# A macaron decoder block on one core: the last pair's sums in place, stores ahead of weights, and three smaller moves of order

## The chip, the cores and the metric

The kernel runs on one core of a Trainium2 chip. The metric is the device time of one execution in microseconds (us). Before the change three executions took 1988.55, 1992.07 and 1992.52 us, so the median is 1992.07. Engines are called PE (TensorE, matmuls), PEld (its weight loads), DVE (VectorE), ACT (ScalarE), POOL (GpSimd) and SP (SyncE, which here issues most DMA transfers).

## The reference

One layer over 1024 tokens of width 1024, all in float32:

```
h = x + 0.5 * swiglu(rms(x), w1a, w3a, w2a)          # hidden width 2816
u = rms(h);  q, k, v, p, gates = split(u @ w_in)     # 3*768 + 512 + 2*1024 columns
yA = dilated_attention(rope(q), rope(k), v) @ w_a    # 12 heads of 64, three dilations
yB = pool(p: trailing means of 2, 4, 8, 16 minus p, per-group map, scale) @ w_b
h = h + (sigmoid(gA) * yA + sigmoid(gB) * yB) @ w_o
h = h + 0.5 * swiglu(rms(h), w1b, w3b, w2b)
out = rms(h)
```

with `swiglu(x) = (silu(x @ w1) * (x @ w3)) @ w2`.

## The kernel before

Every float32 operand of a large product is split into a high part (ACT copies it to the narrower matmul type) and a low part (DVE or POOL subtracts the high part from the original), and each product is three matmuls: high by high, high by low, low by high (`three`). Large products are computed as 2 x 2 blocks by a scheme of seven products instead of eight. `Quad` holds one such block of a weight matrix: `operand(m)` forms the weight sums (lines 343 to 354) and splits them (lines 301 on ACT and 304 on DVE or POOL), `run(m)` issues the 12 matmuls of a product, 2.72 us of PE, in the order 1, 6, 2, 7, 5, 4, 3.

Stages, by the span of the profile: an entry up to 72 us; the up products of the first SwiGLU up to 457; its down products up to 684; an entry, then the projection w_in ("mix") from 723 to 1082; attention with the pool branch and the gates; the product with w_o up to about 1310; then the second SwiGLU, up from 1364 to 1756 and down to 1976.

Up products. A `Pair` is two quads, w1 and w3, for two of the 22 tiles of the hidden width. `a_out` and `b_out` take the finished banks and build silu(a) * b in two tiles of 128 x 1024, y_0 and y_1 (tag `tmp`, three buffers). `finish` then makes the left sums for the down products, y_0 + y_1 (`gb`), two differences (`gd`) and the sum of two halves (`e`), and spills seven pieces of 256 KB to DRAM (`gs_...`). `up` runs ten pairs and then an eleventh whose order is written by hand.

Down products. `Down` runs seven products, each in six steps: five steps of 24 matmuls (5.44 us of PE) and one of 12. `load(i)` (line 610) brings the left sum of step i back from DRAM, into a `tmp` buffer or one of tag `row`; `begin(i)` takes the weights of w2, forms their difference or sum on DVE (line 646, `s_f1w...`), and splits both sides (line 625 on ACT, 629 on DVE or POOL; tiles `bhi`, `blo`, `ahi`, `alo`). `multiply` issues the matmuls (line 663). Steps 0 and 1 are begun at the end of the up products, step 2 is loaded at the start of `Down.run`, and from then on step i loads i + 3 and begins i + 2.

Weights come through one `Stream`, `raws`: seven buffers of 512 KB, loaded in a fixed order by SP (lines 67 and 69). `get` takes the next tile, `back(n)` returns n buffers, which at once issues the next loads. SP issues its transfers in program order, and one that has to wait for its buffer holds up those behind it. Blocks of q, k and v are loaded by four transfers of 128 KB each, one for each index of the first dimension (line 67).

Mix. 19 quads, of kinds qk, v, pool and gate. `Mix.out` takes the finished banks, and for a gate applies the sigmoid (line 947) right behind the vector operation. Small generators, one step per product, do the rest beside the products, in the loop over k: `rotate` and `turn` for q, k and v, `window` for the pooled means, `store` for the gates (line 956), and `split_late`, which splits weights needed later (pool_w, w_a and w_b, w_o; lines 1067 to 1073) and stores the parts to DRAM (line 1077).

At the end of mix SP loads what attention and the pool branch need: q, k, v, gates, and four `pool_in` tiles (line 1547) in the order 2, 3, 0, 1. The pool branch's matmuls are line 1561 (`yp`), in the same order.

W_o. 14 steps. Behind the last sums the residual rows h (`h_again`) are stored to DRAM (line 1878), squared on ACT (line 257), and scaled in place by DVE (line 265), after which PE transposes them (line 379). The first four weights of the second SwiGLU are loaded in the loop at step `STEPS - 5`, by `raws.load()`.

Of the kernel before, what the change touches and what calls it, by code (L numbers as in the profile page):

```python
# [13 lines left out]
OP = mybir.AluOpType  # L14
# [32 lines left out]
class Stream:  # L47
# [7 lines left out]
    def load(self):  # L55
        while self.n_loaded < min(self.end, self.n_back + self.depth):
# [70 lines left out]
def tile_block(  # L127
# [189 lines left out]
    class Quad:  # L317
# [39 lines left out]
        def run(self, m):  # L357
# [8 lines left out]
            if m == 3:  # L366
# [86 lines left out]
    class Pair:  # L453
# [72 lines left out]
        def finish(self):  # L526
# [20 lines left out]
            spill(6, d[:, highs])  # L547
            spill(5, d[:, lows])

    def up(sv, sums, between, at_end, begun):  # L550


        for j in range(NPAIR - 1):
# [15 lines left out]
            q.finish()  # L569
        with tc.manual_schedule():  # L570
# [3 lines left out]
            for k, (w, m, out) in enumerate(items):  # L574
                if k + 2 < n:
                    items[k + 2][0].operand(items[k + 2][1])
                res.append(w.run(m))
# [14 lines left out]
    class Down:  # L592
# [3 lines left out]
        def __init__(self, name, sums, dp):  # L596
            self.name, self.sums, self.dp = name, sums, dp
# [3 lines left out]
            self.half_tile = None  # L601
# [5 lines left out]
        def load(self, i, alloc=tmp):  # L607
# [25 lines left out]
        def begin(self, i):  # L633
            m, s = self.steps[i]
            pr = DOWN[m]
            size = self.size(i)
            for kn in pr.loads:
                self.held[kn, s] = raws.get()
            if len(pr.right) == 1:
                srcs = [self.held[pr.right[0], s]]  # L640
            else:
                x, y, op = pr.right
                srcs = []
                for a in range(size):
                    t = self.half_tile("s", f"w{i}_{a}").rearrange("p (a c) -> p a c", a=1)
                    ve.tensor_tensor(t, self.held[x, s][:, a:a + 1], self.held[y, s][:, a:a + 1], op=op)  # L646
                    srcs.append(t)
            w = self.split("b", srcs, i)
            for kn in pr.drops:
# [1427 lines left out]
```

## Time and profile before

| what | value |
|---|---|
| median of three runs | 1992.07 us |
| profiled execution, its own time | 1990.87 us |
| its span, first to last instruction | 1989.1 us |
| mean granted TensorE clock | 0.991 |
| PE / DVE / ACT / POOL busy | 97% / 67% / 38% / 37% |
| DMA moved | 333.57 MB, mean 168 GB/s |

A window's row gives the stretch, then the busy time of PE, PEld, DVE, ACT and POOL with their instruction counts, then the mean granted clock of PE (1.00 is full speed), the share of time in which the core's 16 DMA engines were busy, and the rate in GB/s. A row of waits names the engine, the tile and line that waited, what ended the wait, and then the total in us, how often, and the longest. "SPq" is SP's queue of transfers. A row of transfers gives the count, the size of one and the median time from issue to landing.

### The profile page before, as it was taken

To read this page: it belongs to the slowest core of one execution; us is meant where nothing else is said; L and a number is where in the kernel's file an instruction comes from. 1 tells how busy PE (TensorE), PEld (TensorE's weight loads), DVE (VectorE), ACT (ScalarE), POOL (GpSimd) and SP (SyncE) were. 2 spreads that over 40 slices of the span, in tenths; PEclk is the share of its full clock that TensorE was granted. 3 is DMA by queue.
4 is the path that set the end of the run, shared out by engine and by line. 5 is a ranking of instruction groups with operands and counts; after the bars stand their busy time and mean duration, and the time that the engine had idled before them with its cause. 6 is when DMAs were issued, how large, how long until landed. Compare 5 with 4: busy or idle time off the path is not lost. (4 is left out here: it accounts for less than half of the span.)

```text
span 1989.1 us, 25124 instructions
## 1 busy us (share of the span) xinstructions
PE 1927.1 (97%) x8966; PEld 1585.2 (80%) x8966; DVE 1334.4 (67%) x2014; ACT 764.0 (38%) x1361; POOL 726.8 (37%) x555
## 2 busy tenths in 40 slices
PE   8999999998999999999998999999999999989997
PEld 7788888886888877788877888877888888868885
DVE  7766556656776775657784786768666556567776
ACT  5333333333344442334445663253323333333343
POOL 4333333331222344444544365534333333322221
PEclk9999999999999999999999999999999999999998
DMA  5323322335466527665668897653333223354664
GB/s 209 126 97 117 117 85 101 133 104 203 140 223 216 196 87 232 219 225 180 230 218 288 229 260 261 260 188 113 120 106 133 80 90 123 126 182 136 205 204 147
DMA packets 147581, 333.57 MB, mean 168 GB/s; under 512 B 20736, under 2 KB 41472, under 8 KB 145920
## 3 DMA queue, kind: packets, MB, share of 16 engines
q1 hardware_dynamic: 139104, 309.12, 46.0%
q10 hardware_dynamic: 8352, 22.85, 3.4%
q8 instruction: 71, 1.16, 0.3%
q14 instruction: 54, 0.44, 0.1%
HBM read 229.61 MB, written 102.30 MB: 167 GB/s over the span
## 5 line engine op out<-in xcount | busy, mean ns | idle before, releaser
L663 PE MATMUL d_f<-bhi_f,ahi_f 128*128 128x512 f32 x616 | 242.4, 393 | 10.4 <-ACT ahi_f L625 8.7
L663 PE MATMUL d_f<-bhi_f,alo_f 128*128 128x512 f32 x616 | 242.3, 393 | 3.0 <-POOL alo_f L629 1.9
L663 PE MATMUL d_f<-blo_f,ahi_f 128*128 128x512 f32 x616 | 241.0, 391 | 0.0
L629 POOL TENSOR_TENSOR alo_f<-g_f,ahi_f 128x512 fp32r<-128x512 f32 x70 | 97.4, 1408 | 317.1 <-ACT ahi_f L625 317.1
L312 PE MATMUL u_mixm<-xhi_t_mix,wc_mixm 128*128 128x512 f32 x608 | 195.4, 392 | 1.4 <-POOL wc_mixm L304 1.3
L312 PE MATMUL u_mixm<-xhi_b_mix,wc_mixm 128*128 128x512 f32 x456 | 150.8, 396 | 6.5 <-DVE y_m L939 5.0
L663 PEld LDWEIGHTS d_f<-bhi_f,ahi_f 128*128 128x128 f32 x616 | 116.6, 189 | 36.5 <-ACT ahi_f L625 10.4
L663 PEld LDWEIGHTS d_f<-bhi_f,alo_f 128*128 128x128 f32 x616 | 116.3, 189 | 31.4 <-POOL alo_f L629 5.4
L663 PEld LDWEIGHTS d_f<-blo_f,ahi_f 128*128 128x128 f32 x616 | 116.4, 189 | 24.0
L312 PEld LDWEIGHTS u_mixm<-xhi_t_mix,wc_mixm 128*128 128x128 f32 x608 | 113.8, 188 | 26.8 <-POOL wc_mixm L304 2.9
L312 PE MATMUL u_mixm<-xlo_t_mix,wc_mixm 128*128 128x512 f32 x304 | 118.4, 389 | 0.0
L304 POOL TENSOR_TENSOR wc_mixm<-s_mixm,wc_mixm 128x512 fp32r<-128x512 f32 x52 | 73.4, 1414 | 102.6 <-ACT wc_mixm L301 90.2
L312 PEld LDWEIGHTS u_mixm<-xhi_b_mix,wc_mixm 128*128 128x128 f32 x456 | 86.3, 189 | 26.9 <-issue 6.8
L312 PE MATMUL u_mixm<-xlo_b_mix,wc_mixm 128*128 128x512 f32 x228 | 89.4, 392 | 0.0
L625 ACT ACTIVATE ahi_f<-g_f 128x1024 fp32r<-128x1024 f32 x84 | 81.8, 974 | 4.9 <-DMA g_f<-gs_f 4.9
L301 ACT ACTIVATE wc_mixm<-s_mixm 128x512 fp32r<-128x512 f32 x76 | 47.0, 629 | 94.5 <-DVE s_mixm L345 45.9
L625 ACT ACTIVATE bhi_f<-s_f2w 128x512 fp32r<-128x512 f32 x55 | 32.9, 628 | 104.3 <-DVE s_f2w L646 96.6
L304 POOL TENSOR_TENSOR wc_mixm<-raw,wc_mixm 128x512 fp32r<-128x512 f32 x40 | 58.8, 1475 | 31.4 <-ACT wc_mixm L301 31.4
L1799 PE MATMUL wo<-w_o,o_hi 128*128 128x512 f32 x224 | 70.2, 395 | 0.0
L625 ACT ACTIVATE bhi_f<-s_f1w 128x512 fp32r<-128x512 f32 x55 | 32.9, 629 | 96.9 <-DVE s_f1w L646 92.2
L312 PEld LDWEIGHTS u_mixm<-xlo_t_mix,wc_mixm 128*128 128x128 f32 x304 | 57.1, 188 | 11.6
L1561 PE MATMUL yp<-pool_in,wab 128*128 128x512 f32 x192 | 52.9, 410 | 5.3 <-DMA pool_in<-pool 5.3
(1297 smaller groups left out, 5091.9 us busy)
## 6 DMA issues: line engine op xcount, KB each, us to landing
g_f<-gs_f SPq DMA_DIRECT2D x70, 512.0 KB, 4.7
raw<-in_w2a_dram SPq DMA_DIRECT2D x35, 512.0 KB, 4.2
raw<-in_w2b_dram SPq DMA_DIRECT2D x35, 512.0 KB, 4.1
raw<-in_w1a_dram SPq DMA_DIRECT2D x22, 512.0 KB, 4.7
raw<-in_w3a_dram SPq DMA_DIRECT2D x22, 512.0 KB, 6.1
gs_f<-y_f SPq DMA_DIRECT2D x44, 256.0 KB, 2.0
gs_f<-gb_f SPq DMA_DIRECT2D x44, 256.0 KB, 2.3
gs_f<-gd_f SPq DMA_DIRECT2D x44, 256.0 KB, 2.8
```

The lines of the kernel that those rows point to most:

```text
L301: ac.activation(w[:, 0], src, AF.Copy)
L304: eng.tensor_tensor(w[:, 1], src, w[:, 0].bitcast(F32), op=OP.subtract)
L312: pe.matmul(p, a, b, start=(start and k == 0 and q == 0), stop=(k == 3 and q == 2), skip_group_check=not start)
L625: ac.activation(hi[:, c], src, AF.Copy)
L629: eng.tensor_tensor(lo[:, d], src[:, o], hi[:, d].bitcast(F32), op=OP.subtract)
L663: pe.matmul(self.banks[m][t], l, r, start=(first and q == 0), stop=(last and q == 2))
L1561: pe.matmul(p, a, b, start=(j == 0), stop=(j == 11))
L1799: pe.matmul(banks[m][t], l, r, start=(st == 0 and j == 0 and q == 0), stop=(st == 1 and j == 1 and q == 2))
```

## The change

Five edits, in both SwiGLUs where they concern the up and down products:

1. `Pair.finish` becomes a generator `parts`. The two differences are made in place in y_0 and y_1, so the tile `gd` goes; the order of the spills is changed. For the last pair it runs inside `Down.run`: its first part behind the matmuls of step 0, its second behind those of step 1, and there `e` is written over half of `gb`, which lives in a pool of its own. The left sums 0 and 1 are loaded at the eighth of the last pair's 14 products, sums 2 and 3 go to buffers of their own (tag `g`), and forming the weight sums is split off (`sums_w`) and called some products before `begin`.
2. The first four weights of the second SwiGLU are loaded behind `step_o(STEPS - 4)`, so behind the stores of the residual rows.
3. The last gate's two stores are issued by ACT.
4. A block of q, k or v is loaded by two transfers of 256 KB.
5. In mix, sigmoids, late splits, gate stores and one operation of the pool windows come one product later.

```diff
-                for q in range(shape[0]):
-                    self.nc.sync.dma_start(a[:, q], src[:, q])
+                for k in range(shape[1]):
+                    self.nc.sync.dma_start(a[:, :, k], src[:, :, k])
...
+        def parts(self, place=None):
...
-            both = row(f"gb_{self.sv.name}{j}")
-            ve.tensor_tensor(both, y[0], y[1], op=OP.add)
-            d = row(f"gd_{self.sv.name}{j}")
-            ve.tensor_tensor(d[:, lows], a21, a11, op=OP.subtract)
-            ve.tensor_tensor(d[:, highs], a12, a22, op=OP.subtract)
-            e = self.sv.half_tile("u", f"{j}5")
-            ve.tensor_tensor(e, a11, a22, op=OP.add)
+            both = (place or row)(f"gb_{self.sv.name}{j}")
             spill(2, a11)
             spill(3, a22)
-            spill(0, e)
+            ve.tensor_tensor(both, y[0], y[1], op=OP.add)
             spill(4, both[:, lows])
             spill(1, both[:, highs])
-            spill(6, d[:, highs])
-            spill(5, d[:, lows])
+            yield
+
+            ve.tensor_tensor(a21, a21, a11, op=OP.subtract)
+            ve.tensor_tensor(a12, a12, a22, op=OP.subtract)
+            spill(6, a12)
+            spill(5, a21)
+            e = both[:, lows] if place else self.sv.half_tile("u", f"{j}5")
+            ve.tensor_tensor(e, a11, a22, op=OP.add)
+            spill(0, e)
...
+                if k == 7:
+                    d.load(0, tmp)
+                    d.load(1, row)
+                if k == n - 4:
+                    d.sums_w(0)
+                if k == n - 2:
+                    raws.back(2)
+                    d.sums_w(1)
+                res.append(w.run(m, k < n - 1))
                 if k == n - 1:
-                    then = at_end(sv.half_tile)
+                    d.dp = room()
+                    d.load(2)
+                    d.begin(0)
                 if k > 0:
                     items[k - 1][2](items[k - 1][1], res[k - 1])
-            then()
+            d.begin(1)
             end.b_out(ORDER[-1], res[-1])
-            end.finish()
+        return d
...
+        def place(self, name):
+            return self.dp.tile([P, 1024], F32, tag="sum", bufs=1, name=name)
+
-        def load(self, i, alloc=tmp):
+        def load(self, i, alloc=None):
+            alloc = alloc or (tmp if i > 3 else lambda n: self.dp.tile([P, 1024], F32, tag="g", bufs=2, name=n))
...
-            self.load(2)
...
+                if i == 1:
+                    next(self.parts, None)
                 if i + 3 < n:
                     self.load(i + 3)
                 if i + 2 < n:
                     self.begin(i + 2)
+                if i == 0:
+                    next(self.parts)
...
                 if gate:
-                    ac.activation(c, c, AF.Sigmoid)
+                    self.then = c
+
+        def activate(self):
+
+            if self.then is not None:
+                ac.activation(self.then, self.then, AF.Sigmoid)
+                self.then = None
...
         def store(self):
-            yield 2
+            yield 3
+
+            queue = nc.sync if self.q < len(MIX) - 1 else nc.scalar
             for a in range(2):
-                nc.sync.dma_start(gate_dram[self.g][:, a], self.y[a])
+                queue.dma_start(gate_dram[self.g][:, a], self.y[a])
...
+                yield 1
                 ve.scalar_tensor_tensor(src[:, w:], src[:, w:], 1.0 / w, y[:, w:], op0=OP.mult, op1=OP.subtract)
                 ve.tensor_tensor(src[:, :w], st[:, :w], y[:, :w], op=OP.subtract)
-                yield 2
+                yield 1
...
         flat = [raws.get() for _ in pieces]
+        yield 1
...
             mix_operand(k + 2)
+            if k - 2 in range(len(items)):
+                mixes[items[k - 2][0]].activate()
...
-            if i == STEPS - 5:
-                raws.end = len(raws.pieces)
-                raws.depth = 4
-                raws.load()
...
         step_o(STEPS - 4)
+        raws.end = len(raws.pieces)
+        raws.depth = 4
+        raws.load()
```

More of the change, by code (lines that the diff above doesn't have):

```diff
@@ L355, in operand, with run @@
             self.w[m] = self.sv.split(src, f"{n}{m}", eng)
-        def run(self, m):
+        def run(self, m, back=True):
             if m not in self.w:
@@ L365, in run @@
             self.sv.product(self.bank[key], w, x, start=m not in (2, 3))
-            if m == 3:
+            if m == 3 and back:
                 raws.back(2)
@@ L639, in begin @@
             if len(pr.right) == 1:
[L640 to L649, printed above, removed]
+                self.right[i] = [self.held[pr.right[0], s]]
+                return
+            x, y, op = pr.right
+            self.right[i] = []
+            for a in range(self.size(i)):
+                t = self.half_tile("s", f"w{i}_{a}").rearrange("p (a c) -> p a c", a=1)
+                ve.tensor_tensor(t, self.held[x, s][:, a:a + 1], self.held[y, s][:, a:a + 1], op=op)
+                self.right[i].append(t)
+        def begin(self, i):
+            m, s = self.steps[i]
+            if i not in self.right:
+                self.sums_w(i)
+            w = self.split("b", self.right.pop(i), i)
+            for kn in DOWN[m].drops:
                 del self.held[kn, s]
-            raws.back(len(pr.drops))
+            raws.back(len(DOWN[m].drops))
             self.ops[i] = (self.split("a", [self.g.pop(i)], i), w)
@@ L843, in tile_block, with down_room, room1 @@
     mstack, dstack = ExitStack(), ExitStack()
-    down = []
     X_mix = {}
-    def begin_down1(half_tile):
+    def down_room(name):
+        return dstack.enter_context(sbuf(f"down_{name}"))
+    def room1():
         scope.close()
         X_mix.update(sums_of_x(mstack.enter_context(sbuf("xa")), "mix", ("b21", "b11")))
-        return begin_down("f1", half_tile)
-    def begin_down(name, half_tile):
-        d = Down(name, sums, dstack.enter_context(sbuf(f"down_{name}")))
-        down.append(d)
-        d.half_tile = half_tile
-        d.load(0)
-        d.begin(0)
-        def then():
-            d.load(1, row)
-            d.begin(1)
-        return then
+        return down_room("f1")
     def load_residual():
@@ L877, in tile_block @@
             begun = begin_up1()
-        up(sv1, sums, load_residual, begin_down1, begun)
+        down = up(sv1, sums, load_residual, "f1", room1, begun)
     raws.depth = RAW_BUFS
@@ L1221, in tile_block @@
         with tc.manual_schedule():
-            down.pop().run(pool, after1, tick)
+            down.run(pool, after1, tick)
     dstack.close()
@@ L1948, in load_residual2 @@
         gains_of.append(load_gain(final_norm, "final"))
-    up(sv2, sums, load_residual2, begin_down2, dict(enumerate(pairs)))
+    down = up(sv2, sums, load_residual2, "f2", room2, dict(enumerate(pairs)))
     fs.close()
@@ L1983, in tile_block @@
         with tc.manual_schedule():
-            down.pop().run(pool, after2)
+            down.run(pool, after2)
     dstack.close()
```

24 lines of the change are left out of this document (13 added, 11 removed).

## The prediction

> **What bounds the kernel now.** I read the page's busy times first, then TensorE's waits, then windows around the places where it waits, then the waits of the queue or engine behind each place.
>
> ```profile
> PE 1927.1 (97%) x8966; PEld 1585.2 (80%) x8966; DVE 1334.4 (67%) x2014; ACT 764.0 (38%) x1361; POOL 726.8 (37%) x555
> ...
> g_f<-gs_f SPq DMA_DIRECT2D x70, 512.0 KB, 4.7
> raw<-in_w2a_dram SPq DMA_DIRECT2D x35, 512.0 KB, 4.2
> ...
> raw<-in_w3a_dram SPq DMA_DIRECT2D x22, 512.0 KB, 6.1
> ...
> gs_f<-gb_f SPq DMA_DIRECT2D x44, 256.0 KB, 2.3
> ```
>
> PE is busy 97% of the span, so at most 62 us can be had without removing matmuls. The change keeps PE's instructions and their order, so I need only ask which of PE's stalls go and which come. TensorE's waits:
>
> ```profile
> PE d_f L663 <- ACT ahi_f L625: 8.7, 4, 5.6
> PE yp L1561 <- DMA pool_in<-pool: 5.3, 2, 5.0
> PE u_mixm L312 <- DVE y_m L939: 5.0, 4, 2.5
> PE x_b L379 <- DVE nst L261: 4.9, 4, 3.5
> ...
> PE d_f L663 <- POOL alo_f L629: 1.9, 3, 0.7
> PE d_f L663 <- DVE u_f L522: 1.8, 2, 1.2
> ```
>
> Five of the six lie where the change works: the down products' first steps (d_f), the pool branch (yp), the mix products (u_mixm), the transposes behind W_o (x_b). A stall costs more than its idle time, which windows show (columns: PE, PEld, DVE, ACT, POOL busy, granted clock, DMA share, GB/s):
>
> ```profile
> 470.00:476.00 6.00, 6.00 (x28) 4.96 (x27) 0.93 (x2) 0.00 (x0) 0.00 (x0) 1.00 0.99 358
> 476.00:482.00 6.00, 0.39 (x2) 0.00 (x0) 2.59 (x4) 2.10 (x3) 0.00 (x0) 0.84 0.93 307
> 482.00:488.00 6.00, 5.82 (x14) 3.72 (x15) 5.28 (x5) 2.21 (x3) 2.96 (x2) 0.59 0.56 199
> ```
>
> ```profile
> 1085.00:1090.00 5.00, 2.94 (x13) 1.70 (x12) 1.84 (x8) 4.63 (x18) 0.00 (x0) 1.00 1.05 378
> 1090.00:1095.00 5.00, 1.27 (x4) 0.62 (x4) 0.00 (x0) 0.00 (x0) 0.00 (x0) 0.61 0.98 321
> ```
>
> ```profile
> 1295.00:1300.00 5.00, 1.75 (x8) 1.13 (x6) 1.12 (x1) 2.45 (x5) 0.52 (x1) 0.93 0.98 380
> 1300.00:1305.00 5.00, 4.78 (x20) 4.49 (x21) 4.53 (x7) 2.39 (x4) 2.05 (x2) 0.50 0.75 309
> ```
>
> After an idle stretch of 3.6 us or more the granted clock is 0.50 to 0.61 and 512-column matmuls start every 0.43 us instead of 0.227. So I count stalls as the excess of PE's start-to-start times over its full-clock cadence, from the trace's list of matmuls: 10.9 us at 457 to 490, 8.6 at 1756 to 1790 (the two handovers from a SwiGLU's up to its down products), 14.5 in the mix products, 5.2 at 1088, 7.9 at 1290 to 1310. Why the first handover starves:
>
> ```profile
> DVE s_f1w L646 <- DMA raw<-in_w2a_dram: 8.4, 2, 7.9
> ```
>
> ```profile
> SPq L610 <- DVE wc_f110b L304: 15.2, 1, 15.2
> SPq L610 <- DVE alo_f L629: 10.4, 2, 6.1
> ```
>
> VectorE waits for weights, because SP's queue stands before the loads of left sums (L610), waiting for buffers that VectorE frees late; the weights behind them are issued at 468.4 to 477.5, all at once.
>
> **Part 1, the handovers.** Loads of sums 0 and 1 now go out seven products earlier, and sum 2 goes into a pool of its own; weights 48 to 51 no longer stand behind sums, sums' buffers and spills. The seven spills and their 1.21 + 3 x 0.68 = 3.3 us of VectorE adds move behind step 0's matmuls. A step is 24 x 0.227 = 5.44 us of PE, which is the cover. I followed the new order with the durations of this trace (VectorE 0.68 for 128x512, ACT 0.63 and 1.04, POOL 1.29 per half, 256 KB landing in 2.3 to 4.4 us, the larger with the queue full): operands of step 0 by 456.3 to 457.8 (PE wants them at 458.2), step 1's by 458.9 (463), step 2's by 464.4 (468.5). Step 3 is late next. The sum `e` now overwrites half of `gb`, so it waits for the landing of the spill issued at about 465.8, at 468.2 to 469.6; behind it on VectorE stands s_f1w3, then blo, then POOL's two halves of alo, at 473.2 and 474.5, against PE's 474.5 and 475.2. That leaves 0 to 1.5 us of stall per handover, and none long enough for the slow clock. I take 1.2 each: 10.9 + 8.6 - 2.4 = 17.1 us gained. Bounds: 19.5 if all goes, 8 if step 3 still waits as long as half of today's.
>
> In regular pairs the differences are made in place, so y_1 of the next pair waits for a spill's landing. From the trace the landing (2.0 us behind its issue) is 2.2 to 4.2 us ahead of the next write in 18 of 20 pairs. In the first handover between pairs of each SwiGLU it is 0.93 us behind it (96.18 against 95.25, 1394.94 against 1394.00). VectorE stands 0.93 us there twice, and PE has banks in hand; I charge 1.1 in all, bounds 0 and 1.9. Sum of part 1: 16.
>
> **Part 2, residual stores ahead of weights.** L265 scales h in place and waits for the store of the same rows:
>
> ```profile
> DVE h_again L265 <- DMA h_dram<-h_again: 4.2, 1, 4.2
> ```
>
> The store is issued at 1289.82 behind 2 MB of weights and lands at 1298.78, when its scale factor has been ready since 1295.0. Ahead of the weights it lands within 2.0 to 4.4 us, by 1294.2, and the scaled row is there at 1295.0 + 1.28 = 1296.3, when PE wants it (1296.37). The second row follows 1.25 us later, some 0.3 of stall. Gone are 3.6 us idle, 1.6 us of slowly clocked transposes (15 starts 0.21 apart instead of 0.11), 1.3 of slow matmuls; less 0.3 and what ACT's copies may hold, 5. Bounds 3.3 (the idle alone, less 0.3) and 6.2. The weights go out 6.5 us later, at about 1293, and land by 1303 at the rate of 380 GB/s; the first is read at 1312.8, so they are still hidden. Without that cover every us would count.
>
> **Part 3, the last gate's stores on ACT's queue.** PE waits at 1088.30 for pool_in0, whose load SP issues at 1084.56 behind two gate stores waiting for the last sigmoid. Now SP issues it at about 1077.5. But the DMA share is 0.98 to 1.05 from 1070 to 1095: pool_in3 lands at 1086.62, the stores' 1 MB at 1089.18, pool_in0 at 1093.69. The bytes are the bound, not the issue. Stores from ACT at 1083.7 share the engines with pool_in3 and pool_in0, and most of their 1 MB still lands before pool_in0. ACT pays two issues of 0.31 to 0.45 ahead of its exps, inside PE's wait. Gain: 1; bounds -0.9 (both issues, nothing else) and 4 (pool_in0 lands 1 MB after pool_in3, 2.8 us, at 1089.5).
> The Trainium skill, "DMA: Bandwidth & Descriptors", section "Issuing engines are not separate DMA queues", speaks against this part: transfers issued by any engine run on the same 16 DMA engines and interleave, so another queue saves issue time alone. By that rule the gain is 0 to 1; by the issue order alone it would be 4; the row of the DMA share agrees with the rule.
>
> **Part 4, mix.** 36 loads of 256 KB replace 72 of 128 KB, and each saves SP an issue of 0.54 to 1.13 us; their tiles land up to 1.2 us earlier. Split weights, pool windows and sigmoids come one product (2.72 us) later. The 17 late pieces then give raw buffers back later; I looked up every load of the gate blocks: landing is 0.4 to 17 us ahead of the first use, and the tightest (landed 1058.6, used 1059.0) waits for the same VectorE instruction as before. So I see no new starving. The stalls are 2.62 at 757.3 (plus 1.6 slow clock), 1.57 at 796.2, and 6.2 in small ones. At 757.3 VectorE's L345 took 1.67 instead of 0.69 us beside POOL's late split, which now moves away; at 796.2 ACT stood behind a late piece not yet landed, which is now a product further. I take half of these 5.8: 3. A VectorE operation costs 1.78 instead of 0.68 us beside POOL wherever the moved pieces now fall, so the bounds are wide: -5 (five collisions of 1 us more, as many as the small stalls before) and +8.
>
> **Sum.** 16 + 5 + 1 + 3 = 25 us. The profiled execution took 1990.87 us (span 1989.1), so 1965.9; the median of the runs, 1992.07, stands 1.2 above it, so 1967.
>
> **The rivals.**
> A, the handovers only half mend: `e`'s wait holds s_f1w3. If the spill lands 7.4 us after its issue, as a store issued at 933.9 did in a full queue, step 3 comes 3 us later, with slow clock 4.5, in both: -9, so 1976. For it: VectorE was full from 455 to 470. Against: the loads are spread now.
> B, moved mix work collides elsewhere: -5 instead of +3, so 1975. For it: POOL's waits in the small stalls (1.3 us) have that cause; against: VectorE is busy 73% of 940 to 1080.
> C, the pool stall goes wholly, 3 us more: 1964. For it the early issue, against it the DMA share.
> D, the other sign: in-place spills hold up y_1 in the 18 regular pairs. They cost nothing while a spill lands within 4.2 us; at A's 7.4 us the pairs lose 7.4 less 2.1 less their margin each, 42 in all, so 2009. From 6.5 us on it eats the whole gain. Against it: 19 of the 20 spills landed in 2.0 to 2.3 us, one in 3.7, and they still stand ahead of the weights.
> E, no change to be seen: stalls return at the next buffer wait, 1991.
>
> **How the numbers follow.** The forecast has 0.56, A 0.15, B 0.12, C 0.07, D 0.05, E 0.05. Faster by over 0.2% (4 us, about what a measurement of this kernel can tell) therefore 0.90, within it 0.05, slower 0.05. All upper bounds together give 1992.07 - 19.5 - 6.2 - 4 - 8 = 1954; all lower ones 1992.07 - 6.1 - 3.3 + 0.9 + 5 = 1989. The range is 1955 to 1985, which holds the forecast, A, B and C.
>
> **What would show it.** Excess at 457 to 490 and 1756 to 1790 under 1.5 us each, and L646 no longer waiting for in_w2a. L265 no longer waiting for h_dram. pool_in0 still landing after the gate stores, PE's wait for it 3 to 5 us. Mix stalls near 11 us. The forecast is wrong if d_f waits for a left sum or s_f1w after a spill, if L485 waits for a gs_f landing in every pair, or if mix stalls exceed 18 us.

## The result and the profile after

The changed kernel takes 1966.82 us (median of four executions, 1965.33 to 1973.42); the kernel before takes 1991.05 us beside it (1988.55 to 1992.52). The ratio is 0.9886, with a 95% interval of 0.9861 to 0.9911. The profiled execution took 1965.33 us, its span is 1963.3 us against 1989.1, and its mean granted clock 0.995 against 0.991.

The page's busy line, and the first rows of TensorE's waits over the whole span:

```profile
PE 1919.7 (98%) x8966; PEld 1581.3 (81%) x8966; DVE 1340.6 (68%) x2014; ACT 762.0 (39%) x1361; POOL 731.8 (37%) x555
```

```profile
PE x_t L379 <- POOL x L432: 3.4, 4, 1.5
PE yp L1591 <- DMA pool_in<-pool: 3.1, 2, 2.7
PE u_mixm L312 <- POOL wc_mixm L304: 2.7, 5, 0.6
PE d_f L689 <- POOL alo_f L651: 1.9, 3, 0.7
PE u_mixm L312 <- DVE y_m L957: 1.7, 2, 1.5
```

PE has the same 8966 matmuls. The longest wait of before, 8.7 us of d_f for ahi_f, is no longer among these rows, and neither is x_b's wait of 4.9 us for nst; the pool branch (yp) still waits 3.1 us for its loads. The windows that answer to those shown of before, in time of this span (handover, pool branch, behind W_o):

```profile
470.00:476.00 6.00, 5.98 (x26) 4.33 (x24) 5.54 (x8) 3.14 (x5) 2.52 (x2) 1.00 0.73 252
476.00:482.00 6.00, 5.29 (x24) 4.36 (x24) 4.28 (x5) 2.92 (x5) 1.76 (x2) 1.00 0.61 222
482.00:488.00 6.00, 6.00 (x29) 4.95 (x28) 2.37 (x3) 2.56 (x4) 0.24 (x1) 1.00 0.92 352
```

```profile
1073.00:1078.00 5.00, 3.71 (x11) 2.12 (x12) 1.37 (x4) 4.48 (x18) 0.00 (x0) 0.66 1.01 419
1078.00:1083.00 5.00, 2.28 (x9) 1.19 (x9) 0.00 (x0) 0.52 (x3) 0.00 (x0) 0.78 1.01 404
```

```profile
1283.00:1288.00 5.00, 5.00 (x31) 4.17 (x30) 4.62 (x7) 3.91 (x7) 2.06 (x3) 1.00 1.01 360
1288.00:1293.00 5.00, 4.18 (x23) 3.14 (x22) 5.00 (x9) 1.20 (x2) 0.00 (x0) 1.00 0.74 303
1295.00:1300.00 5.00, 5.00 (x24) 4.10 (x23) 4.31 (x8) 1.92 (x4) 2.56 (x2) 1.00 0.00 0
```

In the handover PE issues 79 matmuls in these 18 us where it issued 44, at full clock throughout. Behind W_o one gap is left and the clock stays at 1.00. At the pool branch PE still stands, the clock still falls, and the 16 DMA engines are still busy all the time.

To see where the 25.8 us of span come from, I cut the span at the starts of first matmuls of a kind, from the trace's list of matmuls. "Scores" is the stretch from the attention's first scores to the first product behind the pool and attention branches; a further stage of 8.17 us, alike in all kernels, follows it and is left out. The same kernel was profiled once more in a later run (e9 below), and stands here beside the first profile.

| stage, us | before | after | after again |
|---|---|---|---|
| start to first down product (up 1) | 457.73 | 457.66 | 458.18 |
| first handover, down 1, entry, to mix's first product | 226.79 | 217.72 | 217.79 |
| mix | 397.64 | 394.31 | 396.68 |
| scores to the attention's end | 131.77 | 132.01 | 133.88 |
| W_o, entry, up 2 | 534.38 | 529.02 | 529.25 |
| second handover, down 2, to the end | 232.58 | 224.44 | 225.03 |

So 17.2 us (16.5 in the second profile) were gained at the two handovers, and 5.4 (5.1) behind W_o. These repeat. Mix gains 3.3 or 1.0, and the attention loses 0.2 or 2.1: together 3.1 us faster in one execution and 1.1 us slower in the other, with one and the same code.

### The profile page after: what moved, and what is told of

Its sections match the earlier page's. It is cut to its first block, busy times and chain, and to the rows that moved or that the text cites. A ratio compares the mean times of both kernels' runs of the same rounds, so it can differ in the third digit from the quotient of the medians.

```text
span 1963.3 us, 25105 instructions
## 1 busy us (share of the span) xinstructions
PE 1919.7 (98%) x8966; PEld 1581.3 (81%) x8966; DVE 1340.6 (68%) x2014; ACT 762.0 (39%) x1361; POOL 731.8 (37%) x555
## 5 line engine op out<-in xcount | busy, mean ns | idle before, releaser
L312 PEld LDWEIGHTS u_mixm<-xlo_t_mix,wc_mixm 128*128 128x128 f32 x304 | 57.1, 188 | 11.6
```

Source lines behind the costliest of these rows:

```text
L312: pe.matmul(p, a, b, start=(start and k == 0 and q == 0), stop=(k == 3 and q == 2), skip_group_check=not start)
```

## The experiments

My theory after the result: parts 1 and 2 do what the sum says, each by the chain it named; part 3 moves nothing because the bytes in front of the loads, not their issue, set their landing; part 4 is a small gain. The rivals: the handover's gain comes from something else than the spread of loads and spills; the pool branch is held by the order of issue; the later places in mix cost as much as they bring. Each run below was compared with the kernel before on the same chip. The first four shared one chip (before: 1991.63 us), the next four another (1988.45), the last four that one again (1991.88). So the median of one kernel on one chip moved by 3.4 us between two groups of runs.

### e1: part 1 undone

```diff
-        def parts(self, place=None):
+        def finish(self):
...
-                if k == 7:
-                    d.load(0, tmp)
-                    d.load(1, row)
...
-                if i == 0:
-                    next(self.parts)
```

All of `parts`, `sums_w` and the early loads go back to the code of before; parts 2 to 5 of the diff stay.

> The changed kernel with part 1 (both handovers and the sums in place) put back to the old form; the other parts stay. My theory: the handovers alone hold 16 to 17 us of the gain, so 1983 to 1985, with PE's excess over its cadence back at about 10.9 us at the first handover and 8.6 at the second. Rival: the parts help each other (weights or stores of one part in the way of another), so the time is under 1979 or over 1989.

Measured: 1985.62 us (1984.47 to 1986.75), ratio 0.9969 (0.9959 to 0.998). The two stages with the handovers are 227.31 and 233.14 us, 9.6 and 8.7 longer than in the changed kernel: 18.3 us. The time is 0.6 us above the expected range, and the excess of TensorE's starts over its cadence is 11.3 and 9.6 us (10.9 and 8.6 in before). TensorE's waits between 455 and 492 us, and three windows, of this kernel:

```profile
PE d_f L663 <- ACT ahi_f L625: 5.9, 1, 5.9
PE d_f L663 <- DVE u_f L522: 1.2, 1, 1.2
PE d_f L663 <- DVE alo_f L629: 0.4, 1, 0.4
```

```profile
470.00:476.00 6.00, 6.00 (x28) 4.99 (x27) 1.44 (x3) 0.00 (x0) 0.00 (x0) 1.00 1.01 367
476.00:482.00 6.00, 0.93 (x5) 0.43 (x3) 1.92 (x4) 1.29 (x3) 0.00 (x0) 0.94 0.95 301
482.00:488.00 6.00, 4.98 (x10) 3.06 (x11) 4.83 (x6) 3.01 (x4) 2.96 (x2) 0.50 0.50 169
```

The starved stretch, the saturated transfers (share 1.01) and the half clock behind it are all back. Part 1 is worth 17 to 18 us, some 70% of the whole gain.

### e2: part 2 undone

```diff
+            if i == STEPS - 5:
+                raws.end = len(raws.pieces)
+                raws.depth = 4
+                raws.load()
...
         step_o(STEPS - 4)
-        raws.end = len(raws.pieces)
-        raws.depth = 4
-        raws.load()
```

> The changed kernel with the first four weights of the second SwiGLU loaded at the old place again, ahead of the residual stores. My theory: L265 waits about 4 us for the store's landing, the clock falls after 3.6 us of idle PE, and the time is 5 us longer than the changed kernel's 1966.8, so about 1972. Rival: PE was held by ACT's squares or POOL's power as well, so 3 us or less come back (1970 or less).

Measured: 1973.82 us (1970.67 to 1974.83), ratio 0.9906 (0.9889 to 0.9923). The stage from W_o to the second down products is 534.25 us, 5.2 longer than after. VectorE's and TensorE's rows between 1275 and 1320 us:

```profile
DVE h_again L265 <- DMA h_dram<-h_again: 4.4, 1, 4.4
...
DVE nst L261 <- ACT square L257: 1.3, 1, 1.3
```

```profile
PE x_b L379 <- DVE nst L261: 3.7, 1, 3.7
```

The wait for the residual's store is back with the old order (4.4 us, 4.2 before). This profile's span is 9.5 us longer than after, and the other 4.3 lie in stages that the edit does not touch: mix is 2.8 longer, the attention 1.4. e9 shows below that these two vary so by themselves.

### e3, e4, e5: the last gate's two stores at other places

The kernel before stores the last gate from SP, between the second and third load of `pool_in`. The changed kernel stores it from ACT. Three places more:

```diff
 # e3: from SP, behind the four loads of pool_in
-            queue = nc.sync if self.q < len(MIX) - 1 else nc.scalar
+            if self.q == len(MIX) - 1:
+                return
+            queue = nc.sync
...
+        for a in range(2):
+            nc.sync.dma_start(gate_dram[KT - 1][:, a], mixes[-1].y[a])
```

> The changed kernel with the last gate's two stores on SP behind all four pool_in loads, so that their 1 MB moves after pool_in. Theory of bytes: pool_in0 lands 2 to 3 us earlier than in the changed kernel, ACT no longer issues stores ahead of its first exps (1 us), and the wait of 2.9 us at pool_in0 falls to 0.5 to 2: 2 to 5 us faster than 1966.8, so 1962 to 1965. Rival, the wait is the loads' own latency and order: pool_in0 lands when it did, at most the 1 us of ACT's issues is gained, 1966.

```diff
 # e4: from SP, in the program where the changed kernel has them
-            queue = nc.sync if self.q < len(MIX) - 1 else nc.scalar
+            queue = nc.sync
```

> The changed kernel with the last gate's two stores issued by SP again, ahead of pool_in0 and pool_in1 as before the change. Theory of bytes: the queue does not matter, PE waits 5 us for pool_in0 as before the change and saves the 1 us of ACT's issues and the waits before it, so within 1 us of 1966.8. Rival, the early issue is worth something: 2 to 4 us slower, 1969 to 1971.

```diff
 # e5: from SP, in the fifth step of the attention's loop
-            queue = nc.sync if self.q < len(MIX) - 1 else nc.scalar
+            if self.q == len(MIX) - 1:
+                return
+            queue = nc.sync
...
         for q in range(N // 2):
+            if q == 4:
+                for a in range(2):
+                    nc.sync.dma_start(gate_dram[KT - 1][:, a], mixes[-1].y[a])
```

> The changed kernel with the last gate's two stores on SP, issued in attention's fifth step, behind the loads of the second query ring as well. Theory of bytes: at the start of attention the transfers are the bound, and the wait goes to whichever load stands behind the stores' 1 MB (pool_in0, or ACT's wait for the second ring); with the 1 MB moved past both, PE waits under 1.5 us for pool_in and under 1 for ACT, so attention starts 4 to 6 us earlier and the time is 1961 to 1963. Rival: the loads alone saturate the engines, and the time stays at 1966 to 1967.

| | time, us | ratio to before | scores to first yp | yp to first output product | from there to the end | together |
|---|---|---|---|---|---|---|
| before | 1991.05 | | 4.88 | 13.43 | 113.45 | 131.77 |
| after | 1966.82 | 0.9886 (0.9861 to 0.9911) | 5.89 | 12.91 | 113.21 | 132.01 |
| e3, behind pool_in | 1966.80 (1964.43 to 1968.57) | 0.9875 (0.9854 to 0.9895) | 4.98 | 8.60 | 118.08 | 131.66 |
| e4, old place | 1970.89 (1968.72 to 1973.49) | 0.9895 (0.9876 to 0.9914) | 5.29 | 13.97 | 114.52 | 133.78 |
| e5, fifth step | 1964.21 (1962.61 to 1964.82) | 0.9874 (0.9858 to 0.9890) | 5.03 | 11.20 | 115.50 | 131.73 |

With the 1 MB out of the way (e3), the third load of `pool_in`, the one PE waits for, lands 9.2 us after the first scores instead of 11.6, and PE's wait for it shrinks from 2.7 to 0.9 us. But e3 moves more than the bytes: SP also issues that load 1.5 us earlier, 4.5 us ahead of the first scores and not 3.0. In the changed kernel the load goes out 0.06 us behind the landing of a load of v, and further loads, of the next queries, stand in SP's queue until the gate stores that ACT issued have landed:

```profile
SPq L1119 <- DMA gate<-y_m: 5.3, 2, 4.4
...
SPq L1577 <- DMA v_in<-v: 2.4, 2, 1.5
```

From issue to landing the load takes 13.7 us in e3 and 14.5 in the changed kernel, so by this estimate at most 0.8 of the 2.4 us are the 1 MB, and the rest is the earlier issue. In time nothing is gained, where 1962 to 1965 us was expected: of the 5.2 us won up to the first output product 4.9 are lost behind it. ACT's and TensorE's waits of e3 between 1069 and 1100 us:

```profile
ACT ehi L1515 <- PE tp L1503: 5.2, 4, 3.6
ACT qk_hi L1129 <- DMA qk_in<-rot: 4.2, 1, 4.2
```

```profile
PE tp L1503 <- ACT e L1483: 3.4, 3, 2.8
PE yp L1593 <- DMA pool_in<-pool: 0.9, 1, 0.9
```

ACT stands in program order at the split of the next query block, whose load lands 16.7 us behind the first scores, only 0.9 us earlier than in the changed kernel; PE then waits for ACT's exps. In e5 the matmul that the changed kernel issues 69.9 us behind the first scores comes 2.7 us earlier, and fifty matmuls on, at 77.7 us, the lead is 0.3. In that stretch ACT stands at the first split of w_o, behind POOL's sum, which waits for the loads of w_o: 3.8 us in before, 3.5 in after, 4.7 in e5.

So TensorE meets late transfers at several places of the attention, one after the other. That the 1 MB is what costs at the later ones is not shown: ACT stands 4.7 us at w_o in the changed kernel too when it ran again. e5's 1964.21 us lies between its theory's 1961 to 1963 and its rival's 1966 to 1967. In e4 the stores stand behind the first load of `pool_in` and ahead of the other three, since they come a product later than in before, which has two loads on either side. e4's median lies in its rival's range, but so does that of the changed kernel when it ran again (1970.89 too). Against e4 the changed place is 1.8 us shorter in the first profile and 0.1 us longer in the second, so what ACT's queue brings here lies within what the same code varies by.

### e6: part 4's two loads undone

```diff
-                for k in range(shape[1]):
-                    self.nc.sync.dma_start(a[:, :, k], src[:, :, k])
+                for q in range(shape[0]):
+                    self.nc.sync.dma_start(a[:, q], src[:, q])
```

> The changed kernel with four transfers of 128 KB per block of q, k and v again. The mix products took 397.6 us before the change and 394.3 to 397.1 in five profiles that have the new mix code. My theory: the two loads are worth 1 to 2 us of the 3, by letting VectorE start its sums earlier, so the mix products take 396 to 397.5 us and the time is 1967 to 1969. Rival: SP has time to spare and the loads are worth nothing: 394 to 396, time within 1 us of 1966.8.

Measured: 1968.68 us (1967.27 to 1975.57), ratio 0.9906 (0.9879 to 0.9933). Mix is 396.69 us, which is 2.4 more than after and the same as after again. The 256 KB loads bring between 0 and 2.4 us; this run does not settle it.

### e7: late splits, pool windows, gate stores and sigmoids at their old places

```diff
-                    self.then = c
+                    ac.activation(c, c, AF.Sigmoid)
...
-            yield 3
+            yield 2
...
-                yield 1
...
-                yield 1
+                yield 2
...
-        yield 1
         flat = [w.rearrange("p a c -> p (a c)") if len(w.shape) == 3 else w for w in flat]
```

> The changed kernel with late splits, pool windows, gate stores and sigmoids at their old places, a product earlier. My theory: the stall of 1.6 us beside POOL's late split and the one of 1.5 us behind a late piece come back, 2 us of the mix products: 396 to 397.6 us, time 1968 to 1969. Rival: the stalls only moved, the mix products stay at 394 to 396 and the time within 1 us of 1966.8.

Measured: 1963.37 us (1961.13 to 1969.26), ratio 0.9876 (0.9853 to 0.9898), some 5 us under the expected time. Mix is 396.02 us, within what the new places give. Its stalls changed places: the one near 748 us is 2.61 again instead of 1.64, the one of 1.67 near 995 is back, and the two of 1.51 and 0.80 near 782, which came with the new places, are gone. The stall behind a late piece, 1.57 us near 796 us of before, does not come back with the old places; of the mix edits e7 keeps the two loads, which were not tried alone with these places. The surprise is the attention: 128.22 us, 3.8 less than after. The stretch from yp to the first output product is 7.28 instead of 12.91. SP's queue around the end of mix, in before, after and e7:

```profile
SPq L956 <- ACT y_m L947: 8.2, 1, 8.2
SPq L1077 <- ACT raw L1072: 4.5, 1, 4.5
```

```profile
SPq L1105 <- ACT raw L1100: 6.9, 1, 6.9
```

```profile
SPq L1103 <- ACT raw L1098: 4.5, 1, 4.5
```

In before SP stands longest at the last gate's stores, waiting for the sigmoid, with loads of `pool_in` behind them; that wait is gone in both others. What is left is the store of the last late piece, which waits for ACT's split of it, 4.5 us at the old place and 6.9 at the new one. Behind it in the same queue are a gate's two stores, two loads of v, w_a and w_b, a gate, and the four loads of `pool_in`. With the old places the first of the late piece's two stores goes out 15.46 us ahead of the first scores (before: 15.46) and not 13.51, and the third load of `pool_in` is issued 6.7 us ahead of them and not 3.0. In e7 TensorE does not wait for `pool_in`; PEld waits 0.3 us for it and VectorE 0.2. The third load lands 7.7 us behind the first scores, ahead of both gate stores (9.9 and 12.6).

So the old places shorten the pool branch's wait: PE waits 2.1 to 3.5 us for `pool_in` in the six profiles with the new places and the stores on ACT (after, e1, e2, e6, e8, e9), and 0, 1.1 and 0 us in the three with the old places and the stores on ACT (e7, e10, e12). Moved a product later, these pieces take back what the gate stores' move to ACT gains. That it is the late split among them follows from SP's queue, but it was not run alone. The attention takes 128.22, 130.62 and 131.39 us in the three, mean 130.1, and 132.01 to 135.68 in the six, mean 133.4. How much of this is the granted clock is said under e9.

### e8: the last sum behind begin(3)

```diff
             spill(5, a21)
+            if place:
+                yield
             e = both[:, lows] if place else self.sv.half_tile("u", f"{j}5")
...
                 if i == 0:
                     next(self.parts)
+                if i == 1:
+                    next(self.parts, None)
```

> The changed kernel with the last pair's sum e, which waits for a spill's landing, moved behind the operands of step 3 on VectorE. My theory: VectorE no longer stands 1.0 us ahead of s_f1w3, the operands of step 3 come 1.0 to 1.7 us earlier, and step 3's stall of 0.9 to 1.1 us goes in both handovers: excess at each handover 0.4 to 0.7 us instead of 1.4 to 1.8, 2 us in all, 1965. Rival: POOL's halves beside VectorE's operations are what makes step 3 late (1.73 us instead of 1.29), and the stalls stay over 0.7 us.

Measured: 1966.61 us (1963.88 to 1968.16), ratio 0.9886 (0.9869 to 0.9903). The handovers' excess falls from 1.8 and 1.4 us to 0.4 each, and their stages are 1.30 and 0.95 us shorter: 2.2 us. VectorE's waits between 440 and 490 us, in after and then in e8:

```profile
DVE blo_f L651 <- ACT bhi_f L647: 5.8, 4, 3.1
...
DVE gb_f L551 <- DMA gs_f<-gb_f: 1.0, 1, 1.0
```

```profile
DVE blo_f L653 <- ACT bhi_f L649: 4.9, 5, 2.6
```

The wait for the spill's landing is gone, and with it PE's stall. The rival falls: POOL's two halves take 1.53 and 1.74 us here too, but they start 1.6 us earlier, the 0.97 of the wait and the 0.6 of the sum itself. The time does not show the gain, since in this profile the attention took 135.68 us, 3.7 more than in the first profile of the same attention code; ACT stood 5.4 us at the split of w_o.

### e9 to e12: the changed kernel again, and three joined versions

e9 is the changed kernel without an edit. e10 is e7 with e8's edit; e11 is e10 with e5's; e12 is e7 with the sigmoids as in the changed kernel, thus:

```diff
 # e12, against the changed kernel
-            yield 3
+            yield 2
...
-                yield 1
...
-                yield 1
+                yield 2
...
-        yield 1
         flat = [w.rearrange("p a c -> p (a c)") if len(w.shape) == 3 else w for w in flat]
```

> The changed kernel once more, beside the three that follow, so that they are compared with it on one chip. If the stage lengths of one code repeat, the mix stage is 394.3 us and the stretch from the attention's first scores to its end 132.0 us, as in the first profile of it. If they drift by themselves, as the same mix code gave 394.3 to 397.1 us in seven kernels and the same attention code 131.7 to 135.7, one of the two is off by 1 us or more. Time 1964 to 1969 us.

> Late splits, pool windows, gate stores and sigmoids at their old places, and the last sum behind begin(3). If the two are independent, it takes 3.4 us less than the changed kernel by the first and 2.2 us less by the second: 1958.5 to 1962 us, with the handovers' excess 0.3 us each and 128 us from the first scores to the attention's end. If the second's gain is given back at the attention's start whatever the cause, as in the kernel with the late sum alone, that stretch is 131 us or more and the time is that of the old places alone, 1961 to 1964.

> As the run before it, and the last gate's two stores go out in the attention's fifth step. If the stores' 1 MB is what the pool products still wait for, the stretch from first scores to first output product shrinks from 13 to 11 us or less and the time by 1 to 2 us. If the old places already freed that wait (the pool products waited for no load there), nothing is left to gain, and the 1 MB meets the loads of w_o at 67 us into the attention instead: 0 to 2 us longer.

> Old places for the late splits, pool windows and gate stores, the sigmoids a product later as in the changed kernel. If the moved sigmoids are what shortens the mix products, that stage is 394.3 to 395 us and the stretch from the first scores to the attention's end 128 us: time 1961 to 1963. If the moved splits and windows are what shortens it, the stage stays at 396 us, the 747 us stall is back at 2.6 us, and the time is 1963 to 1965.

| | time, us | ratio to before | mix | scores to the attention's end | the two handover stages |
|---|---|---|---|---|---|
| e9, changed kernel | 1970.89 (1966.13 to 1973.74) | 0.9892 (0.9868 to 0.9916) | 396.68 | 133.88 | 442.82 |
| e10 | 1963.92 (1962.56 to 1967.30) | 0.9863 (0.9841 to 0.9886) | 395.20 | 130.62 | 439.90 |
| e11 | 1963.53 (1962.91 to 1967.94) | 0.9864 (0.9841 to 0.9886) | 396.46 | 133.50 | 440.66 |
| e12 | 1962.95 (1962.15 to 1963.85) | 0.9856 (0.9835 to 0.9877) | 393.20 | 131.39 | 442.28 |

e9 misses its expected time by 2 us, and answers its question: two profiles of one code differ by 2.4 us in mix and by 1.9 in the attention, and its median lies 4 us above the first one's. Over all profiles of one code mix varies by 2.9 us and the attention by 3.7. So no smaller difference of these stages is shown by one pair of profiles, while the first handover (217.72 and 217.79), W_o (529.02 and 529.25) and the second handover (224.44 and 225.03) can be read to some tenths.

Part of this spread is the granted clock. The first 30 us from the first scores on, in after, e9, e7 and e12:

```profile
1069.70:1099.70 30.00, 25.26 (x154) 19.70 (x153) 15.99 (x59) 17.83 (x54) 5.08 (x4) 0.83 0.95 317
```

```profile
1072.65:1102.65 30.00, 25.32 (x149) 19.01 (x149) 15.99 (x59) 17.84 (x54) 5.06 (x4) 0.77 0.95 311
```

```profile
1071.10:1101.10 30.00, 27.99 (x189) 22.28 (x189) 19.91 (x74) 20.45 (x64) 5.05 (x4) 0.94 0.94 309
```

```profile
1068.50:1098.50 30.00, 27.82 (x194) 22.50 (x193) 19.95 (x75) 20.45 (x64) 5.05 (x4) 0.94 0.90 288
```

A mean of 0.83 over 30 us is 10.2 us at a clock of 0.50; e9 has 13.7 us of it, e7 and e12 have 3.4. Over the whole attention the clock is at 0.50 for 6.8 to 17.1 us in the six profiles with the new places named under e7, and for 3.4 to 6.8 in the three with the old ones. If half of that time is lost, which is an estimate from the clock's record and the most it can be, the means are 6.0 and 2.8 us. The difference, 3.1 us, is about that of the attention's means, 3.3. So a wait at the pool branch seems to cost mostly by the slow clock that comes with it. In mix the clock fell for 3.4 us behind the stall near 782 us in e9 and not at all in the first profile: by the same estimate 1.7 of their 2.4 us.

The three versions with the old places of the late splits, windows and gate stores, and e7 before them, have the four lowest medians of all, 1962.95 to 1963.92 us, but e5 follows at 1964.21, and by the ratio to before e3 and e5 (0.9875 and 0.9874) stand level with e7 (0.9876). e12's four executions all lie under the nine of the changed kernel. In e10 the late sum again shortens the handover stages (by 1.8 us against e7's 441.67) but adds nothing to e7's time; the last gate's stores in the fifth step (e11) bring nothing either. Neither theory of e11 came out as it stood: PE still waits 1.1 us for `pool_in` in e10 and 2.4 in e11, the stretch to the first output product is 15.2 us and not 11, and the attention's 2.9 us over e10's lie within what one code varies by.

In e12, of these pieces, the sigmoids alone stand at their new place. Mix is 393.20 us, the shortest of all fourteen profiles, and the 748 us stall is 2.62 us, that is, not mended. In length alone this is one profile, and e10, whose clock stayed at 1.00 in mix as e12's did, is 2.0 us longer. But the stalls repeat. In the four profiles with the old sigmoids (before, e7, e10, e11) PE stands near 1006 us of before's span (995 in the others) for ACT's copy of a bank, which stands behind a sigmoid that waits 2.2 us for VectorE: 1.67 us of excess. In the ten with the new ones that wait is not there, and a stall of 0.8 to 1.2 us for a split on POOL is what is left near it. TensorE's row of before, between 994 and 1009 us:

```profile
PE u_mixm L312 <- ACT y_m L928: 1.5, 1, 1.5
```

The splits, windows and gate stores of the changed kernel gain and lose: near 748 us the stall is 1.64 instead of 2.62 in all nine profiles that have them (10 us later in e1), and near 782 us each of the nine has stalls of 2.2 to 2.9 us, which e7, e10, e11 and e12 do not have. So of the mix edits it is the sigmoids that help.

e12 also shows where the rest of the lead goes. TensorE waits for no `pool_in` in it, and the matmul that the changed kernel issues 69.9 us behind the first scores comes 5.3 us earlier. Fifty matmuls on the lead is 0.6 us, and TensorE's first row of the whole span is now a new one:

```profile
PE tp L1499 <- ACT e L1479: 5.1, 3, 3.1
```

```profile
ACT w_o L1347 <- POOL w_o_in L1344: 6.5, 1, 6.5
```

The second row is ACT's in the stretch from 1125 to 1150 us: 6.5 us at the first split of w_o, where the changed kernel stands 3.5 (4.7 in e9). Behind it the clock is at 0.50 for 3.4 us. The loads of w_o land 2.1 us earlier than in the changed kernel where PE is 5.3 us ahead; in e7 they land 3.8 us earlier, and its lead of 3.8 us stays. That the loads of w_o would have to go out sooner follows from this, but was not tried.

## Why the prediction was right, and where its terms were off

The predicted 1967.0 us stands against 1966.82 measured, and 1970.89 when the same kernel ran again; the forecast's case is the one that came. That the sum came so near is in part luck, since parts 3 and 4 differ by 4 us between two profiles of the same kernel. By its own steps:

**Part 1, sum 16.** Right in mechanism and size: 17.2 and 16.5 us by the stages, 18.3 by undoing it. The chain came as written, somewhat later: VectorE's timeline at the first handover has

```profile
466.09 1.22 DVE L541 TENSOR_TENSOR gb_f<-y_f,y_f 128x1024 f32<-128x1024 f32 x1
467.34 0.69 DVE L546 TENSOR_TENSOR y_f<-y_f 128x512 f32<-128x512 f32 x1
467.95 0.69 DVE L547 TENSOR_TENSOR y_f<-y_f 128x512 f32<-128x512 f32 x1
469.61 0.69 DVE L551 TENSOR_TENSOR gb_f<-y_f,y_f 128x512 f32<-128x512 f32 x1 [0.97 <-DMA gs_f<-gb_f]
470.22 1.29 DVE L667 TENSOR_TENSOR s_f1w<-raw,raw 128x512 f32<-128x512 f32 x2
471.97 1.30 DVE L651 TENSOR_TENSOR blo_f<-s_f1w,bhi_f 128x512 fp32r<-128x512 f32 x2 [0.46 <-ACT bhi_f L647]
```

`gb` was added at 466.09, so its spill left at about 467.3 and not 465.8, and `e` started at 469.61, behind a landing foreseen by 469.6 at the latest. POOL's two halves took 1.54 and 1.73 us beside VectorE, not 1.29. PE's excess was 1.78 and 1.41 us where 1.2 each was taken; the first is 0.3 over the 1.5 that was named as the limit. That `e`'s wait is what remains was argued then and is shown by e8. (The bound of 8 does not follow from its words: half of 19.5 leaves 9.7.)
The charge of 1.1 us for y_1 was too high: no cost is seen. The two waits named exist, but are 0.34 and 0.38 us and not 0.93 (at 96 us the spill lands at 96.11 and the write starts at 96.19), PE has banks in hand, and the up products take 457.66 us, and 458.18 in e9, against 457.73.

**Part 2, sum 5.** Right: 5.4 and 5.1 by the stages, 5.2 by undoing it, between the bounds of 3.3 and 6.2. L265 no longer waits for h_dram; its waits between 1270 and 1300 us are two for nst, 0.8 us in all. The weights were hidden as foreseen.

**Part 3, sum 1.** The size is near (the wait for `pool_in` fell by 2.2 us, the start of yp came 1.0 later, and the stage as a whole changed by +0.2 and +2.1), but the step "the bytes are the bound, not the issue" is only half true. (ACT's two issues were hidden, as foreseen: PE stands 1.3 us at its first transposes for ACT's exps, and then still has to wait for the load.) The third load lands 11.6 us behind the first scores, between the two gate stores (9.3 and 13.1), as it landed at 11.5 in the kernel before, which issued it 5.4 us later. But in the nine profiles with the stores on ACT it lands 13.9 to 15.1 us behind its issue, wherever that is: issued 6.7 us ahead of the first scores (e7) and not 3.0, it lands at 7.7, in front of the gate stores, and PE does not wait. So rival C, "the pool stall goes wholly", comes true in e7 and e12, where part 4's late pieces do not push SP's queue back, and in e10 but for 1.1 us. Its 3 us more are not shown: the attention of these three is 3.6, 1.2 and 0.4 us shorter than in the one profile of before.
The Trainium skill, "DMA: Bandwidth & Descriptors", section "Issuing engines are not separate DMA queues", says that issuing from several engines saves issue time alone. With the new places the trace agrees (131.7 to 133.9 us wherever the stores go); with the old places it agrees only if the issue time that is saved counts the loads that stood behind the stores: SP waited 8.2 us for the last sigmoid in the kernel before.

**Part 4, sum 3.** This is the term that failed, in its step "I see no new starving". I followed each late piece's buffers to the loads of the gate blocks, but not the store of the last piece in SP's queue and what stands behind it: the transfers of the next stage. By the means under e7 that costs the attention some 3.3 us, the clock included. In mix itself 3.3 and 1.0 us were gained, against 3 predicted, but only in part as told. Of the two collisions that were to go, the one at 757 us of before went as told: with the slow clock behind it, it had 4.3 us of excess and has 1.8 in both profiles. The one at 796, 1.7 us before, came back at 782 with 2.7 and 4.5. Some 1.1 us came near 1006 us, from the moved sigmoids (e12), which the sum did not price. Near 782 us ACT stood 7.5 us, not for a late piece but at its own issues of `rotate`'s stores. In ACT's timeline, rows of ACTq are issues, and x2 joins the ones at 774.86 and 780.36:

```profile
774.86 5.81 ACTq L991 DMA_DIRECT2D rot<-y_m  x2
782.42 0.34 ACTq L993 DMA_DIRECT2D qk<-y_m  x1
782.87 0.63 ACT L301 ACTIVATE wc_mixm<-raw 128x512 fp32r<-128x512 f32 x1 [7.51 <-DMA rot<-y_m]
```

The last two issues, at 780.36 and 782.42, went out 0.02 us behind the landing of an earlier transfer each (a load of weights, a store of v). The landing of `rot` that the last row names had come at 779.74, before both. Counted alike over the mix products from 723 us of before on, the stalls are 13.0 us before, 9.6 after and 12.0 in e9, where the sign was "near 11"; the prediction's 14.5 does not agree with its own list, which adds up to 12.0.

The stall at 782 us is a collision of rival B's kind, smaller than the one it priced.

So parts 3 and 4 were to bring 4 us and brought 3.1 in one profile and lost 1.1 in the other; parts 1 and 2, at 22.6 and 21.7 against 21, carried the forecast. Rival A fell (the spill landed after some 2.3 us, not 7.4), D fell (the two waits of L485 named under part 1 are in the first handover between pairs; in the 18 regular pairs none is for a spill's landing, and up 1 is as long as before), and E fell.

## What to carry to other kernels

When one edit moves work later inside a stage, follow its last instance to the end of the stage: the queue in which its store stands also issues the first loads of the next stage, and their landing can decide more than the stall that was mended. Price a wait of TensorE with the slow clock behind it. Where the transfers are saturated for tens of us, a wait that goes at one place can come back at the next load in that stretch (third pool_in, next queries, w_o), so sum the whole stretch before booking a gain. The starved handovers here, by contrast, were mended by spreading their loads over the work ahead of it, and the gain can be read from stage lengths that repeat to some tenths of a us.

## What was unexpected of the hardware

- With the DMA engines fully busy, an earlier issue can bring nothing: the third `pool_in` load was issued 5.4 us earlier than in before and landed at the same time (11.5 and 11.6 us behind the first scores). Issued another 3.7 us earlier (e7), it landed 3.8 us earlier.
- Issuing from another engine did not part the queues: ACT's stores at 780.36 and 782.42 us went out 0.02 us behind the landing of other transfers, and SP stood up to 4.4 us until stores issued by ACT had landed.
- The same code's stages are not alike in how they repeat. Up 1 lies between 457.6 and 458.3 us in all fourteen profiles, but mix of one code (but for the last gate's stores) between 394.26 and 397.12 in eight, and the attention of one code between 132.01 and 135.68 in six. Part of it is the clock, which is at 0.50 for none or 3.4 us of mix and for 6.8 to 17.1 us of the attention; behind the same stall of 2.6 us near 748 us it fell in e7 and e11, and not in e10 and e12. Why it differs was not settled.
- The granted clock fell without a long idle stretch. In e7 TensorE's longest wait at the pool branch is 1.4 us, but it was sparsely used (0.97 and 1.46 of 2 us) ahead of the fall:

```profile
1073.00:1075.00 2.00, 0.97 (x7) 0.59 (x6) 1.68 (x10) 1.51 (x2) 0.00 (x0) 1.00 0.99 406
1075.00:1077.00 2.00, 1.46 (x6) 0.80 (x7) 0.07 (x1) 1.90 (x9) 0.00 (x0) 0.85 1.01 358
1077.00:1079.00 2.00, 2.00 (x7) 1.62 (x6) 1.05 (x2) 1.59 (x6) 0.00 (x0) 0.50 1.00 420
```
